# Batched row gather on one core: direct indices, six gather buffers, repeated rows left out and expanded on TensorE

## The chip, the core and the metric

The kernel runs on one core of one Trainium2 chip. A core has five engines with their own instruction queues: PE (TensorE, matrix multiplication), DVE (VectorE), ACT (ScalarE), POOL (GpSimd) and SP (SyncE), and 16 DMA engines that move data between HBM and the on-chip memory SBUF. SP, ACT and POOL can start DMA transfers; a gather by a list of row numbers is started by POOL. Matrix products land in PSUM, from which DVE and ACT copy them to SBUF. The metric is the time of one launch in microseconds (us) on the device; lower is better.

## The reference: what is computed

```python
def setup_inputs():
    batch, seq, dim = 32, 512, 1024
    return {
        "x": np.random.randn(batch, seq, dim).astype(np.float32),
        "indices": np.random.randint(0, seq, (batch, 128)).astype(np.int32),
    }

def reference(x, indices):
    for b in range(batch):
        result[b] = x[b, indices[b]]
```

For each of 32 batches, 128 rows of 1024 float32 values (4 KB each) are picked out of the batch's 512 rows and written in order. Indices are drawn with repetition, so a batch usually names some rows more than once. The launch hands the indices over as 64-bit integers. Nothing is calculated: 16.8 MB are read and 16.8 MB are written.

## The kernel before

One SBUF pool, `tp`, gives every tile name four buffers. The start: SP loads all indices transposed (L15), so that partition n holds the n-th index of every batch; these are 4096 separate elements of 8 bytes. DVE takes the low 32 bits (L17). POOL writes the row offsets 0, 512, 1024, ... with an iota (L20), and DVE adds them (L21), so that `idx2` holds row numbers in the flattened input of 32 x 512 rows.

Then a loop over the batches (L25). For each, POOL issues an indirect DMA (L27) that fetches 128 rows, one to a partition, into `buf` (128 x 1024 float32, 512 KB), and a plain DMA (L31) writes `buf` to the output. The writes alternate between SP's queue (even batches) and ACT's queue (odd batches). In the profile the gathers are queue q0, SP's DMAs q1, ACT's q10.

The tile framework derives the waits. A write waits for its gather to land. A gather waits until the write that last read its buffer, four batches earlier, has landed. Every engine goes through its queue in order, so on POOL the gather of batch 4 waits for the write of batch 0, and all later gathers stand behind it. No engine computes in the loop.

Of the kernel before, what the change touches and what calls it, by code (L numbers as in the profile page):

```python
# [5 lines left out]


@with_exitstack
def kernel(ctx, tc, x, indices, out):
    nc = tc.nc  # L10
    B, S, D = x.shape
    N = indices.shape[1]
    tp = ctx.enter_context(tc.tile_pool(name="sbuf", bufs=4))
    idx = tp.tile([128, B], dtype=indices.dtype)
    nc.sync.dma_start(out=idx[:], in_=indices[:, :].rearrange("b n -> n b"))  # L15
    idx32 = tp.tile([128, B], dtype=mybir.dt.int32)
    nc.vector.tensor_copy(out=idx32[:], in_=idx[:].bitcast(mybir.dt.int32)[:, ::2])  # L17
    idx2 = tp.tile([128, B], dtype=mybir.dt.int32)
    iota = tp.tile([128, B], dtype=mybir.dt.int32)
    nc.gpsimd.iota(iota[:], pattern=[[S, B]], base=0, channel_multiplier=0)  # L20
    nc.vector.tensor_tensor(out=idx2[:], in0=idx32[:], in1=iota[:], op=mybir.AluOpType.add)  # L21
    xf = x.flatten_outer_dims()
    of = out.flatten_outer_dims()
    engs = [nc.gpsimd, nc.sync, nc.scalar]
    for b in range(B):  # L25
        buf = tp.tile([N, D], dtype=x.dtype)
        nc.gpsimd.indirect_dma_start(  # L27
            out=buf[:], out_offset=None,
            in_=xf[:], in_offset=bass.IndirectOffsetOnAxis(ap=idx2[:, b:b+1], axis=0),
        )  # L30
        engs[1 + b % 2].dma_start(out=of[b*N:(b+1)*N], in_=buf[:])  # L31


# [1 line left out]
_INS = ['x', 'indices']  # L35
_OUTS = [((32, 128, 1024), 'float32')]


def kernel(**inputs):
    import numpy as _np  # L40
    import concourse.bacc as _bacc
    import concourse.tile as _tile
    from concourse import mybir as _mybir
    from concourse.bass_utils import run_bass_kernel_spmd as _run

    nc = _bacc.Bacc("TRN2", target_bir_lowering=False, num_devices=1)  # L46
    arrays, args = {}, []
    for name in _INS:
        a = _np.ascontiguousarray(inputs[name])
        if a.dtype.kind in "iu":  # L50
            a = a.astype(_np.int64)
        arrays[f"in_{name}_dram"] = a
        args.append(nc.dram_tensor(f"in_{name}_dram", a.shape, _mybir.dt.from_np(a.dtype), kind="ExternalInput").ap())
    for i, (shape, dtype) in enumerate(_OUTS):
        dt = _mybir.dt.from_np(_np.dtype(dtype))
        args.append(nc.dram_tensor(f"out_{i}_dram", shape, dt, kind="ExternalOutput").ap())
    with _tile.TileContext(nc) as tc:  # L57
        kernel(tc, *args)
    r = _run(nc, [arrays], core_ids=[0])
    got = tuple(r.results[0][f"out_{i}_dram"] for i in range(len(_OUTS)))  # L60
    return got[0]
```

## Time and profile before

| what | value |
|---|---|
| median of 4 runs | 112.43 us (109.51 to 113.75) |
| the profiled execution's own time | 111.54 us |
| its span, first to last instruction | 109.8 us |
| POOL busy | 30.5 us, of which 32 gathers at 943 ns |
| DVE busy | 0.4 us |
| moved by DMA | 33.60 MB, 306 GB/s over the span |
| gather, from issue to landing (median) | 6.0 us |
| write, from issue to landing (median) | 5.7 us (SP), 5.1 us (ACT) |
| index load, from issue to landing | 4.0 us |

How to read the lines that follow: "busy" counts an engine's own work, without the issuing of DMAs and without waits. In the row of DMA digits the span is cut into 40 slices, and each digit is the mean busy share of the 16 DMA engines in tenths. A DMA queue's line gives packets, megabytes, and the time its packets took as a share of 16 engines over the span; a gathered or written row of 4 KB is one packet, and each transfer ends with one small packet per DMA engine, 16 in all. A wait is named by who waited, for whom, and then total, times and longest. All of it comes from one profiled execution.

### The profile page before, as it was taken

What the parts mean: (1) busy time and instruction counts of PE and PEld (TensorE: products, weight loads), DVE (VectorE), ACT (ScalarE), POOL (GpSimd) and SP (SyncE); (2) the same over time, 40 slices, a digit from 0 to 9 for tenths busy, and PEclk for the clock granted to TensorE, in tenths of its full rate; (3) what the DMA queues carried; (4) which work ended last, traced back from release to release, by engine and by line L of the source; (5) the groups of instructions that cost most, each with busy time, mean ns of one, the idle gap of its engine ahead of it and who ended that gap; (6) DMA issues with size and microseconds to landing.
All of it is one profiled execution on the core that took longest, in us unless ns stands there. A gap on an engine that the chain in (4) does not pass through costs nothing.

```text
span 109.8 us, 173 instructions
## 1 busy us (share of the span) xinstructions
DVE 0.4 (0%) x2; POOL 30.5 (28%) x37
## 2 busy tenths in 40 slices
DVE  0100000000000000000000000000000000000000
POOL 1076003730075003720066001740037200660000
DMA  2529999899989899899989899788998999989991
GB/s 4 8 31 318 275 412 388 263 370 397 419 257 349 227 394 402 248 303 381 421 290 352 246 372 405 212 334 230 403 405 242 267 342 418 361 258 370 419 397 54
DMA packets 13329, 33.60 MB, mean 306 GB/s; under 512 B 5136, under 2 KB 5136, under 8 KB 13328
## 3 DMA queue, kind: packets, MB, share of 16 engines
q0 software_dynamic: 4608, 16.78, 48.0%
q1 hardware_dynamic: 6416, 8.42, 20.7%
q10 hardware_dynamic: 2304, 8.39, 18.7%
q14 instruction: 1, 0.01, 0.0%
HBM read 16.81 MB, written 16.78 MB: 306 GB/s over the span
## 4 chain that ended last, share of the span: by engine, by line
DMA 79%; issue 7%; POOLq 2%; POOL 1%; DVE 0%; DVEq 0%
DMA out_dram<-buf 42%; DMA buf<-in_x_dram,idx 33%; DMA idx<-in_indices_dram 4%; POOLq L57 1%; POOL buf L27 1%; DVE idx L21 0%; DVE idx L17 0%; POOLq L27 0%; DVEq L21 0%
## 5 line engine op out<-in xcount | busy, mean ns | idle before, releaser
L27 POOL DMA_INDIRECT buf<-in_x_dram,idx x32 | 30.2, 943 | 67.2 <-DMA out_dram<-buf 54.7
L20 POOL IOTA iota<- 128x32 int32 x1 | 0.1, 145 | 0.4 <-PEq L57 0.4
L17 DVE COPY idx<-idx 128x32 int32<-128x32 int32 x1 | 0.2, 181 | 4.8 <-DMA idx<-in_indices_dram 4.8
L21 DVE CUSTOM_DVE_ANT_0 idx<-idx,iota 128x64 uint16<-128x64 uint16 x1 | 0.2, 194 | 0.1
L46 POOL MEMSET const-float32-0.0<- 128x1 f32 x1 | 0.1, 100 | 0.2 <-issue 0.2
L46 POOL MEMSET const-uint8-127<- 128x1 uint8 x1 | 0.1, 120 | 0.0
L46 POOL MEMSET const-bfloat16-1.0<- 128x1 bf16 x1 | 0.1, 114 | 0.0
L46 POOL MEMSET const-float32-1.0<- 128x1 f32 x1 | 0.1, 106 | 0.0
## 6 DMA issues: line engine op xcount, KB each, us to landing
out_dram<-buf SPq DMA_DIRECT2D x16, 512.0 KB, 5.7
out_dram<-buf ACTq DMA_DIRECT2D x16, 512.0 KB, 5.1
buf<-in_x_dram,idx POOLq DMA_INDIRECT x32, 6.0
idx<-in_indices_dram SPq DMA_DIRECT2D x1, 32.0 KB, 4.0
```

Source lines behind the costliest of these rows:

```text
L17: nc.vector.tensor_copy(out=idx32[:], in_=idx[:].bitcast(mybir.dt.int32)[:, ::2])
L20: nc.gpsimd.iota(iota[:], pattern=[[S, B]], base=0, channel_multiplier=0)
L21: nc.vector.tensor_tensor(out=idx2[:], in0=idx32[:], in1=iota[:], op=mybir.AluOpType.add)
L27: nc.gpsimd.indirect_dma_start(out=buf[:], out_offset=None, in_=xf[:], in_offset=bass.IndirectOffsetOnAxis(ap=idx2[:, b:b+1], axis=0),)
L46: nc = _bacc.Bacc("TRN2", target_bir_lowering=False, num_devices=1)
L57: with _tile.TileContext(nc) as tc:
```

## The change

The changed kernel moves the same rows in another way.

- The indices are loaded in three forms. `idx0` is the first batch's list alone (128 elements). `v4` is the whole table in four quarters of 32 batches x 32 positions, two on SP's queue and two on ACT's; DVE takes the low halves (`low`) and transposes each 32 x 32 block, which gives `idxT` with a batch per column. `v` is the table with a batch per partition.
- A gather takes its row numbers straight from these; the batch's place in the input is a constant `element_offset`, so no iota of offsets is added.
- Six gather buffers `U` are used in turn. Batches 0 to 5 (`HEAD`) are gathered whole and written from `U`, alternating between SP and ACT.
- From batch 6 on, `prep` handles four batches at a time. TensorE broadcasts a batch's index list to all partitions (`bc`). DVE compares it with each partition's own index and counts equal entries at lower positions (even batches) or higher positions (odd batches) in `cnt`; `lead` marks positions whose count is zero. Other positions get 65536 added to their row number (`at`), which is out of bounds, and the gather is told to leave such rows out. `s` is a 128 x 128 matrix of zeros and ones that maps each kept row to every position that names it.
- Two matmuls of 512 columns multiply the gathered rows by `s` into PSUM (`ps`, three buffers), DVE copies the first half and ACT the second into `block`, and SP writes the block. Each of the 26 blocks has its own place in SBUF. A buffer of `U` comes free when its matmuls have read it.

The instruction order of the built program has the broadcasts of batches 6 to 25 ahead of the first expansion on PE, those of 26 to 29 after block 17 and those of 30 and 31 after block 21. ACT's copy of a block waits for DVE's. All writes from batch 6 on are in SP's queue.

```diff
--- before.py
+++ after.py
@@ -4,31 +4,125 @@
 from concourse import mybir
 from concourse._compat import with_exitstack
 
+F32 = mybir.dt.float32
+I32 = mybir.dt.int32
+ALU = mybir.AluOpType
 
 @with_exitstack
 def tile_coalesced_load_kernel(ctx, tc, x, indices, out):
     nc = tc.nc
     B, S, D = x.shape
     N = indices.shape[1]
-    tp = ctx.enter_context(tc.tile_pool(name="sbuf", bufs=4))
-    idx = tp.tile([128, B], dtype=indices.dtype)
-    nc.sync.dma_start(out=idx[:], in_=indices[:, :].rearrange("b n -> n b"))
-    idx32 = tp.tile([128, B], dtype=mybir.dt.int32)
-    nc.vector.tensor_copy(out=idx32[:], in_=idx[:].bitcast(mybir.dt.int32)[:, ::2])
-    idx2 = tp.tile([128, B], dtype=mybir.dt.int32)
-    iota = tp.tile([128, B], dtype=mybir.dt.int32)
-    nc.gpsimd.iota(iota[:], pattern=[[S, B]], base=0, channel_multiplier=0)
-    nc.vector.tensor_tensor(out=idx2[:], in0=idx32[:], in1=iota[:], op=mybir.AluOpType.add)
+    HEAD, GRP, FAR = 6, 4, 65536
+    const = ctx.enter_context(tc.tile_pool(name="const", bufs=1))
+    ring = ctx.enter_context(tc.tile_pool(name="ring", bufs=1))
+    rows = ctx.enter_context(tc.tile_pool(name="rows", bufs=1))
+    pick = ctx.enter_context(tc.tile_pool(name="pick", bufs=1))
+    junkp = ctx.enter_context(tc.tile_pool(name="junk", bufs=2))
+    pbc = ctx.enter_context(tc.tile_pool(name="pbc", bufs=2, space=bass.MemoryType.PSUM))
+    pout = ctx.enter_context(tc.tile_pool(name="pout", bufs=3, space=bass.MemoryType.PSUM))
+    idx0 = const.tile([N, 1], indices.dtype, name="idx0")
+    nc.sync.dma_start(out=idx0[:], in_=indices.rearrange("b n -> n b")[:, 0:1])
+    v4 = const.tile([N, 32], indices.dtype, name="v4")
+    for q in range(4):
+        (nc.scalar if q % 2 else nc.sync).dma_start(
+            out=v4[32 * q:32 * q + 32, :], in_=indices[:, 32 * q:32 * q + 32])
+    v = const.tile([B, N], indices.dtype, name="v")
+    nc.scalar.dma_start(out=v[:], in_=indices)
+    diff = const.tile([N, N], I32, name="diff")
+    nc.gpsimd.iota(diff[:], pattern=[[1, N]], base=0, channel_multiplier=-1)
+    idxT = const.tile([N, B], I32, name="idxT")
+    lo = v4[:].bitcast(I32).rearrange("p (n two) -> p n two", two=2)[:, :, 0]
+    low = const.tile([N, B], I32, name="low")
+    nc.vector.tensor_copy(out=low[:], in_=lo)
+    nc.vector.transpose(out=idxT[:], in_=low[:])
+    idxF = const.tile([N, B], F32, name="idxF")
+    nc.vector.tensor_copy(out=idxF[:], in_=idxT[:])
+    vf = const.tile([B, N], F32, name="vf")
+    nc.vector.tensor_copy(
+        out=vf[:], in_=v[:].bitcast(I32).rearrange("p (n two) -> p n two", two=2)[:, :, 0])
+    ident = const.tile([N, B], F32, name="ident")
+    nc.vector.tensor_scalar(out=ident[:], in0=diff[:, :B], scalar1=0, scalar2=None, op0=ALU.is_equal)
+    other = []
+    for k, op in enumerate((ALU.is_lt, ALU.is_gt)):
+        m = const.tile([N, N], F32, name=f"other{k}")
+        nc.vector.tensor_scalar(out=m[:], in0=diff[:], scalar1=0, scalar2=None, op0=op)
+        other.append(m)
     xf = x.flatten_outer_dims()
     of = out.flatten_outer_dims()
-    engs = [nc.gpsimd, nc.sync, nc.scalar]
-    for b in range(B):
-        buf = tp.tile([N, D], dtype=x.dtype)
+    def gather(dst, at, b, **kw):
         nc.gpsimd.indirect_dma_start(
-            out=buf[:], out_offset=None,
-            in_=xf[:], in_offset=bass.IndirectOffsetOnAxis(ap=idx2[:, b:b+1], axis=0),
-        )
-        engs[1 + b % 2].dma_start(out=of[b*N:(b+1)*N], in_=buf[:])
+            out=dst[:], out_offset=None,
+            in_=xf[:], in_offset=bass.IndirectOffsetOnAxis(ap=at, axis=0),
+            element_offset=b * S * D, **kw)
+    U = [ring.tile([N, D], F32, name=f"u{k}") for k in range(HEAD)]
+    for b in range(HEAD):
+        gather(U[b], idx0[:].bitcast(I32)[:, 0:1] if b == 0 else idxT[:, b:b + 1], b)
+        (nc.sync if b % 2 == 0 else nc.scalar).dma_start(out=of[b * N:(b + 1) * N], in_=U[b][:])
+    cnt = const.tile([N, B], F32, name="cnt")
+    lead = const.tile([N, B], F32, name="lead")
+    far = const.tile([N, B], F32, name="far")
+    at = const.tile([N, B], I32, name="at")
+    spread = {}
+    def prep(g0):
+        g1 = min(g0 + GRP, B)
+        bc = pbc.tile([N, GRP * N], F32, name="bc")
+        for b in range(g0, g1):
+            nc.tensor.matmul(bc[:, (b - g0) * N:(b - g0 + 1) * N],
+                             lhsT=ident[:B, b:b + 1].to_broadcast([B, N]), rhs=vf[:],
+                             start=True, stop=True)
+        for b in range(g0, g1):
+            junk = junkp.tile([N, N], F32, name="junk")
+            nc.vector.scalar_tensor_tensor(
+                out=junk[:], in0=bc[:, (b - g0) * N:(b - g0 + 1) * N], scalar=idxF[:, b:b + 1],
+                in1=other[b % 2][:], op0=ALU.is_equal, op1=ALU.mult, accum_out=cnt[:, b:b + 1])
+        w = slice(g0, g1)
+        nc.vector.tensor_scalar(out=lead[:, w], in0=cnt[:, w], scalar1=0.0, scalar2=None, op0=ALU.is_equal)
+        nc.vector.tensor_scalar(out=far[:, w], in0=cnt[:, w], scalar1=0.0, scalar2=float(FAR),
+                                op0=ALU.is_gt, op1=ALU.mult)
+        nc.vector.tensor_tensor(out=at[:, w], in0=far[:, w], in1=idxF[:, w], op=ALU.add)
+        for b in range(g0, g1):
+            s = pick.tile([N, N], F32, name=f"s{b}")
+            nc.vector.tensor_scalar(
+                out=s[:], in0=bc[:, (b - g0) * N:(b - g0 + 1) * N], scalar1=idxF[:, b:b + 1],
+                scalar2=lead[:, b:b + 1], op0=ALU.is_equal, op1=ALU.mult)
+            spread[b] = s
+    starts = list(range(HEAD, B, GRP))
+    done = 0
+    for b in range(HEAD, B):
+        while done < len(starts) and starts[done] <= b + 2 * GRP:
+            prep(starts[done])
+            done += 1
+        u = U[b % HEAD]
+        gather(u, at[:, b:b + 1], b, bounds_check=S - 1, oob_is_err=False)
+        ps = pout.tile([N, D], F32, name="ps")
+        for h in range(2):
+            nc.tensor.matmul(ps[:, h * 512:(h + 1) * 512], lhsT=spread[b][:],
+                             rhs=u[:, h * 512:(h + 1) * 512], start=True, stop=True)
+        block = rows.tile([N, D], F32, name=f"block{b}")
+        nc.vector.tensor_copy(out=block[:, :512], in_=ps[:, :512])
+        nc.scalar.copy(out=block[:, 512:], in_=ps[:, 512:])
+        nc.sync.dma_start(out=of[b * N:(b + 1) * N], in_=block[:])
 
 
 # ---- launch: one core; inputs and outputs as the reference has them ----
```

## Prediction

> **What bounds the kernel now.** I read the head of the page and its engine shares first, then the queues, the waits, and two-microsecond windows of the DMA traffic.
>
> ```profile
> span 109.8 us, 173 instructions
> ...
> DVE 0.4 (0%) x2; POOL 30.5 (28%) x37
> ...
> DMA  2529999899989899899989899788998999989991
> ...
> q0 software_dynamic: 4608, 16.78, 48.0%
> q1 hardware_dynamic: 6416, 8.42, 20.7%
> q10 hardware_dynamic: 2304, 8.39, 18.7%
> ...
> HBM read 16.81 MB, written 16.78 MB: 306 GB/s over the span
> ```
>
> No engine computes: POOL is 28% busy, and the row of DMA digits is near 9 from the fourth slice on. The DMA engines are the resource. q0 is the gathers, q1 SP's writes (and the index load), q10 ACT's writes. The same 16.78 MB cost 48.0% of the span as gathers, 52.7 us, and twice q10's 18.7%, 41.0 us, as writes. A gathered row of 4 KB took 0.480 x 109.8 x 16 / 4096 = 206 ns of a DMA engine, a written row 160 ns. Why: in the packet records of the trace both have a median of 159 ns, but 345 of the 4096 gather packets took over 300 ns; what they took above 159 ns is 174.6 us on 16 engines, 10.9 us of the span.
>
> ```profile
> POOL buf L27 <- DMA out_dram<-buf: 54.7, 9, 8.5
> POOL buf L27 <- issue: 7.9, 22, 0.6
> DVE idx L17 <- DMA idx<-in_indices_dram: 4.8, 1, 4.8
> ```
>
> These are waits: total, times, longest. POOL stands 54.7 us until a write has landed and frees one of four buffers, so four gathers go out together, then four writes. The windows (length, DVE, POOL, clock, DMA share, GB/s) show what that does:
>
> ```profile
> 10.00:12.00 2.00, 0.00 (x0) 0.45 (x1) 1.00 0.94 291
> 14.00:16.00 2.00, 0.00 (x0) 0.00 (x0) 1.00 1.02 418
> 20.00:22.00 2.00, 0.00 (x0) 1.38 (x3) 1.00 0.81 246
> 28.00:30.00 2.00, 0.00 (x0) 0.00 (x0) 1.00 1.03 420
> ```
>
> 10 to 12 is gathers alone, 291 GB/s at a share of 0.94. At 20 to 22 a new set of gathers starts: 246. 28 to 30 is writes alone, 420. The decisive one is 14 to 16; its queues:
>
> ```profile
> q0 software_dynamic: 112, 0.42, 51.4%
> q1 hardware_dynamic: 80, 0.29, 35.5%
> q10 hardware_dynamic: 30, 0.12, 14.9%
> ```
>
> Half of its bytes are gathers, the total is 418, and a gather packet took 0.514 x 2000 x 16 / 112 = 147 ns. Beside writes, gathers move at the writes' pace; alone they don't.
>
> The span: the first gather packet starts at 7.4 us, the last write packet ends 1.7 us before the end, gathers and writes take 93.7 us, so 109.8 - 7.4 - 1.7 - 93.7 = 7.0 us are holes.
>
> [...]
>
> **The change, part by part.**
>
> *Index load.* Now: issue at 0.74, 4096 packets of 8 bytes, landing at 4.79, two DVE steps, gather 0 at 5.62. After: 128 packets on SP first. The old packets started at 1.83, ran to 4.23 and landed 0.56 later; with a 32nd of the packets landing is at about 1.83 + 0.08 + 0.56 = 2.5, and gather 0 issues at 2.6, with no DVE step. Its first packet follows 1.8 us later as now (5.62 to 7.42): 4.4 instead of 7.4, minus 3.0 us. Gathers 1 to 5 need the transposed indices. The four quarter loads stand second and third on SP's queue and first and second on ACT's (0.43 us an issue), land by about 3.5, and then low, vf and transpose take three DVE steps of about 0.2 us; vf stands ahead of the transpose and waits for ACT's third load. About 4.3, against a POOL free at 2.6 + 1.39 = 4.0: cost 0 to 0.5 us, hidden by gather 0's 0.5 MB in flight.
>
> *Overlap.* Six buffers, and after the head a buffer comes free when its matmuls have read it, not when a write has landed. POOL's back-to-back pace is 1.24 us a gather (7.01 to 8.26), a block needs at least 2.5 us of DMA, so gathers run ahead and both kinds of packets are queued throughout. Gather packets then cost between 160 ns (writes' pace) and 206 ns (their present mean). I take about 178, a third of the way up, since the mixed window gave 147 but its gathers had been issued long before. Holes: bounds 0.5 and 7.0; I take 3.0, because while the first six buffers wait for their writes (gather 6 waits for write 0) there is a second short spell of gathers alone.
>
> *Skipped rows.* Counted in the input, batches 6 to 31 repeat 364 rows of 3328, so 3732 gather packets stay: 3732 x 160 / 16 = 37.3 us at least, 52.7 x 3732 / 4096 = 48.0 at most; at 178 ns 41.5. Writes stay at 41.0. [...] The bounds check on POOL is in no row: from nothing to a doubling of the 0.94 us; 2.2 us a gather still fits in a block's 2.5.
>
> *Expansion.* [...] All of this is hidden while gathers lead by six buffers and three PSUM tiles; [...] it shows once, behind the last gather, where queued writes still fill the DMA engines. New waits: PE waits for a gather with later matmuls and the last groups' broadcasts behind it; DVE's copy waits for PE with later groups' masks behind it; SP waits for ACT's copy with all later writes behind it. None is due within a block's time, as the broadcasts of batches 6 to 25 stand ahead of the first expansion.
>
> Sum: 4.4 + 41.5 + 41.0 + 3.0 + 1.2 + 1.7 = 92.8 us of span. The profiled execution took 111.54 for 109.8, 1.7 around the span: **94.5 us**. The median of the runs, 112.43, is 0.9 above the profiled one, within their spread of 4.2, so I add nothing.
>
> **Rivals.**
> *Gathers keep their own pace*, 206 ns and all holes: 4.4 + 48.0 + 41.0 + 7.0 + 1.2 + 1.7 = 103.3, 105.0 us. For it: the slow packets come with new gathers, also at 20 to 22. Against: the mixed window.
> *The skip saves nothing*, the packets being moved all the same, or POOL paying for the check: 364 packets x 178 / 16 = 4.0 more, 98.5 us. Nothing in the profile speaks on it.
> *TensorE sets the pace, cold.* Gather 0 lands at 2.6 + 4.4 = 7.0, write 0 5.7 later, gather 6 issues at 13.4 and lands at 19.4 (6.0). [...]
>
> **Chances.** 0.62 the forecast, 0.17 own pace, 0.09 no saving, 0.09 cold TensorE, 0.03 in between. Two per cent is about what a measurement of this kernel can tell from no change. Faster 0.87, same 0.04, slower 0.09. Low end: 4.4 + 37.3 + 41.0 + 0.5 + 1.2 + 1.7 = 86.1, 87.8 with the surround. High end: own pace and a little, 106; [...].
>
> **What would show it.** Right: the first gather packet near 4.4 us, GB/s digits near 400 without the swing, q0 at about 3732 plus 512 packets, POOL waiting for PE or for nothing after the head. Wrong: [...] q0's share above 46 us; q0 still at 4608 packets; POOL's gathers above 2.2 us.

## The result and the profile after

The changed kernel takes 91.9 us (median, 90.12 to 93.1) against 111.81 us for the kernel before; the ratio is 0.823, with a 95% interval of 0.812 to 0.834. The forecast was 94.5 us, with a range of 87.5 to 106.0. Medians take in a kernel's slow executions and ratios do not (the fast ones of the changed kernel took 90.1 to 91.4 us), so differences are given both ways below, a hundredth of the ratio being 1.1 us. The profiled execution took 92.8 us for a span of 90.9 us.

The page of the changed kernel: span, the rows of DMA share and of GB/s in 40 slices, and the queues.

```profile
span 90.9 us, 704 instructions
...
DMA  0189999999998998999999999999999999999760
GB/s 5 24 240 247 297 396 387 414 418 405 411 395 227 353 232 321 416 420 416 420 418 420 414 418 420 422 416 416 422 413 418 418 420 418 418 418 398 321 277 18
...
q0 software_dynamic: 4608, 15.29, 45.9%
q1 hardware_dynamic: 4416, 15.22, 41.1%
q10 hardware_dynamic: 576, 1.62, 4.5%
```

From the seventeenth slice on, the swing between 250 and 420 GB/s of the kernel before is gone: the row stands at 413 to 422 for some 45 us. Two weak places are left, the start up to 297, and a spell with 227, 353, 232 and 321 between 27 and 36 us.

In the queues, q0 carries 15.29 MB instead of 16.78. The difference, 1.49 MB, is 364 rows of 4 KB, so the skipped rows are really not moved. But q0 still has 4608 packets. In the packet records 3732 of them have 4 KB, and 876 have 4 bytes and take 9 ns: the 512 that end the transfers, as before, which leaves just one for each of the 364 skipped rows. A skipped row leaves a tiny packet in its place.

The waits of the changed kernel (who waited for whom: total, times, longest):

```profile
POOL u L70 <- PE ps L120: 24.1, 19, 2.0
...
PE ps L120 <- DMA u<-in_x_dram,at: 12.3, 15, 5.2
...
POOL u L70 <- DMA out_dram<-u: 6.2, 4, 2.9
POOL u L70 <- DVE at L102: 5.0, 1, 5.0
```

POOL's 54.7 us behind writes have become 6.2. It now waits 24.1 us for TensorE, never over 2.0 at a time: the ring of six is full, and POOL takes the next buffer as soon as matmuls have read it. Most of that costs nothing, because the DMA engines have work: 418 GB/s from 36 us on. The last line is one to distrust. It belongs to gather 6, issued at 15.27 us, and DVE had finished `at` for it at 8.44; what came last was the landing of write 0, which held the same buffer.

The windows (length, PE, weight loads, DVE, ACT, POOL, clock, DMA share, GB/s) say where the span goes:

```profile
4.00:10.00 6.00, 4.32 (x18) 4.03 (x19) 4.04 (x25) 0.00 (x0) 4.43 (x5) 1.00 0.83 225
10.00:26.00 16.00, 8.42 (x28) 5.99 (x27) 7.71 (x44) 1.28 (x1) 5.26 (x6) 1.00 1.01 397
26.00:36.00 10.00, 10.00 (x21) 4.35 (x20) 5.77 (x17) 2.43 (x5) 5.53 (x6) 1.00 0.90 291
36.00:80.00 44.00, 37.14 (x87) 13.70 (x85) 16.76 (x42) 11.02 (x19) 15.23 (x16) 1.00 1.03 418
```

At 26 to 36 us the DMA engines move 291 GB/s instead of 418. That is (418 - 291) x 10 / 418 = 3.0 us lost, while TensorE works for 10.00 of 10 us. The worst two microseconds of the spell, as a window and as its queues:

```profile
28.00:30.00 2.00, 2.00 (x4) 0.73 (x4) 0.60 (x5) 0.37 (x1) 0.99 (x1) 1.00 0.68 154
```

```profile
q0 software_dynamic: 100, 0.31, 67.9%
```

No write packet moves there, and the gather packets that do belong to gathers issued at 24.31 and 26.99 us.

### The profile page after: what moved, and what is told of

The parts are those of the page before. It is cut to its first block, busy times and chain, and to the rows that moved or that the text cites. A ratio compares the mean times of both kernels' runs of the same rounds, so it can differ in the third digit from the quotient of the medians.

```text
span 90.9 us, 704 instructions
## 1 busy us (share of the span) xinstructions
PE 64.3 (71%) x156; PEld 29.4 (32%) x156; DVE 36.9 (41%) x132; ACT 16.5 (18%) x27; POOL 32.0 (35%) x37
## 3 DMA queue, kind: packets, MB, share of 16 engines
q0 software_dynamic: 4608, 15.29, 45.9%
HBM read 16.84 MB, written 16.78 MB: 370 GB/s over the span
## 4 chain that ended last, share of the span: by engine, by line
issue 39%; DMA 34%; POOL 15%; PE 2%; DVE 2%; POOLq 1%; SPq 1%; ACT 1%; DVEq 0%
POOL u L70 15%; DMA u<-in_x_dram,at 13%; DMA u<-in_x_dram,idxT 12%; DMA out_dram<-u 7%; PE ps L120 2%; DMA v<-in_indices_dram 2%; POOLq L70 1%; DVE block L123 1%; ACT block L124 1%; SPq L39 0%; SPq L36 0%; DVE low L51 0%; POOLq L151 0%; DVE idxT L52 0%; DVE idxF L54 0%
## 5 line engine op out<-in xcount | busy, mean ns | idle before, releaser
L120 PE MATMUL ps<-u,s 128*128 128x512 f32 x104 | 52.7, 640 | 12.9 <-DMA u<-in_x_dram,at 12.3
L70 POOL DMA_INDIRECT u<-in_x_dram,at x26 | 25.7, 989 | 36.1 <-PE ps L120 24.1
L123 DVE COPY block<-ps 128x512 f32<-128x512 f32 x26 | 18.0, 691 | 41.1 <-PE ps L120 41.1
L120 PEld LDWEIGHTS ps<-u,s 128*128 128x128 f32 x104 | 19.1, 200 | 44.6 <-issue 37.1
L124 ACT COPY block<-ps 128x512 f32<-128x512 f32 x26 | 15.2, 585 | 49.4 <-DVE block L123 45.7
L90 PE MATMUL bc<-vf,ident 32*128 32x128 f32 x52 | 11.8, 398 | 8.0 <-DVE ident L59 4.4
L90 PEld LDWEIGHTS bc<-vf,ident 32*128 32x128 f32 x52 | 10.3, 291 | 10.4 <-DVE ident L59 4.4
L95 DVE SCALAR_TENSOR_TENSOR junk<-bc,idxF,other 128x128 f32<-128x128 f32 x26 | 7.9, 347 | 4.4 <-PE bc L90 4.0
L105 DVE TENSOR_SCALAR s<-bc,idxF,lead 128x128 f32<-128x128 f32 x26 | 9.5, 405 | 0.0
L70 POOL DMA_INDIRECT u<-in_x_dram,idxT x5 | 4.7, 947 | 1.7 <-issue 1.2
```

Of the source, the lines that this page charges most:

```text
L70: nc.gpsimd.indirect_dma_start(out=dst[:], out_offset=None, in_=xf[:], in_offset=bass.IndirectOffsetOnAxis(ap=at, axis=0), element_offset= ...
L90: nc.tensor.matmul(bc[:, (b - g0) * N:(b - g0 + 1) * N], lhsT=ident[:B, b:b + 1].to_broadcast([B, N]), rhs=vf[:], start=True, stop=True)
L95: nc.vector.scalar_tensor_tensor(out=junk[:], in0=bc[:, (b - g0) * N:(b - g0 + 1) * N], scalar=idxF[:, b:b + 1], in1=other[b % 2][:], op0= ...
L105: nc.vector.tensor_scalar(out=s[:], in0=bc[:, (b - g0) * N:(b - g0 + 1) * N], scalar1=idxF[:, b:b + 1], scalar2=lead[:, b:b + 1], op0=ALU. ...
L120: nc.tensor.matmul(ps[:, h * 512:(h + 1) * 512], lhsT=spread[b][:], rhs=u[:, h * 512:(h + 1) * 512], start=True, stop=True)
L123: nc.vector.tensor_copy(out=block[:, :512], in_=ps[:, :512])
```

## The experiments

My theory was the forecast's: gathers and writes queued side by side make most of the gain, the index path gives 3 us, the skipped rows give 4 us, and the expansion is hidden. The rivals: the skipped rows and the start make the gain; or gathers keep their own pace, whatever runs beside them.

**A buffer for every batch, nothing else.**

```diff
+    bp = ctx.enter_context(tc.tile_pool(name="blocks", bufs=B))
-        buf = tp.tile([N, D], dtype=x.dtype)
+        buf = bp.tile([N, D], dtype=x.dtype)
```

> The kernel before with one change: every batch has a buffer of its own, so that no gather waits for a write. If the gain is made by gathers and writes being queued side by side, gather packets fall from 205 ns to about 177 and the holes go: 7.4 + 4096 x 177 / 16000 + 40.8 + 2.4 + 1.7 = 97.6 us of span, some 99 us, ratio 0.88. If gathers keep their own pace whatever runs beside them, only the holes go: 7.4 + 52.4 + 40.8 + 2.4 + 1.7 = 104.7, some 106 us, ratio 0.95. If the gain is made by the skipped rows and the index path, no change.

Measured: 94.34 us, ratio 0.861 (0.849 to 0.874). Most of the whole gain comes from a buffer count. A gather packet takes 167 ns on average instead of 205 (packet records), less than the 177 I expected, and packets over 300 ns are down from 345 to 62. POOL no longer waits for writes; it waits 30.2 us, in 20 waits, for earlier gathers to land, with about six in flight.

**Eight buffers instead of four, nothing else.** The same edit with `bufs=8`.

> The kernel before with one change: eight gather buffers instead of four. If lead is what counts and eight suffice (a gather took 6.0 us and a write 5.7 in the kernel before, together 4.7 blocks of 2.5 us): close to the kernel with a buffer for every batch, which took 94.3 us, say 96 us, ratio 0.88. If gathers and writes still go out in turn, now eight by eight: the holes are halved and the gather packets stay slow, 105 us, ratio 0.95.

Measured: 94.33 us, ratio 0.857 (0.846 to 0.868), as fast as with a buffer for every batch. Its page and its longest wait:

```profile
span 92.3 us, 169 instructions
...
GB/s 2 13 0 206 281 261 400 398 423 419 423 419 417 417 424 424 414 423 417 423 421 417 421 421 423 419 417 417 424 421 417 421 419 423 419 419 417 423 382 21
```

```profile
POOL buf L28 <- DMA out_dram<-buf: 37.6, 23, 3.4
```

POOL still waits 37.6 us for writes, but in 23 waits of at most 3.4 us, where four buffers gave 9 waits of up to 8.5. Eight buffers let POOL issue most gathers long before their rows move: 12.4 us from issue to landing by the median, where four gave 6.0. Neither a resident output nor a skipped row is needed for this part.

Is it the writes beside them that make the gathers quick, as the forecast had it, or the time since they were issued? The packet records tell. With the packets taken in order, 144 to a gather, all 345 slow packets (over 300 ns) of the kernel before moved within 6 us of their gather's issue, and of the 83 that moved within 3 us of it beside at least two write packets in motion 67 were slow. With eight buffers, 282 gather packets moved 8 us or more after the issue with no write, or one write packet, in motion: 159 ns on average, none slow. So a gather issued long before needs no writes beside it, and a quite fresh one is slow in spite of them; what writes add for packets between 3 and 6 us is not clear from these records. Why a fresh gather has slow packets no run here shows.

**The index path alone**, with four buffers.

```diff
-    nc.sync.dma_start(out=idx[:], in_=indices[:, :].rearrange("b n -> n b"))
...
+    nc.sync.dma_start(out=idx0[:], in_=indices.rearrange("b n -> n b")[:, 0:1])
...
+    nc.vector.transpose(out=idxT[:], in_=low[:])
...
+                ap=idx0[:].bitcast(I32)[:, 0:1] if b == 0 else idxT[:, b:b + 1], axis=0),
+            element_offset=b * S * D,
```

> The kernel before with the new index path alone (first batch's list first, the others transposed on DVE, constant element offset), four buffers as before. If the start counts one to one: 3.0 us less, some 109 us, ratio 0.973. If the start is hidden or given back by the order of four gathers and four writes: no change, ratio 1.00.

Measured: 109.21 us, ratio 0.970 (0.961 to 0.979), 2.6 us less by the medians and 3.3 by the ratios. The start counts about one to one.

**Both together**, no skipping and no expansion.

> Both of the two before together: a buffer for every batch and the new index path, no row left out and nothing expanded. If the two add up: some 96 us, ratio 0.86; the skipping and expanding of the changed kernel is then worth some 4 us net. Rival: the expansion costs as much as the skipped rows save, and this kernel is as fast as the changed one, 92 us, ratio 0.82.

Measured: 91.46 us, ratio 0.833 (0.819 to 0.846). The two parts about add up, and here my theory took its first blow: this kernel, which has neither masks nor matmuls, can't be told from the changed one (0.823, 0.812 to 0.834). The difference of a hundredth lies inside the intervals. Either the skip saves nothing, or the expansion costs what it saves.

**The changed kernel without the skip.**

```diff
-    HEAD, GRP, FAR = 6, 4, 65536
+    HEAD, GRP, FAR = 6, 4, 0
```

> The changed kernel with FAR = 0: repeated rows are gathered all the same, everything else is kept, the masks, the matmuls and the copies too. If a skipped row saves its packet: 364 packets x 177 / 16000 = 4.0 us more than the changed kernel, 95.9 us. If the DMA engines are not the bound there, or a skipped row costs as much as a fetched one: no change, 91.9 us.

Measured: 94.79 us, ratio 0.859 (0.831 to 0.888): 2.9 us more than the changed kernel by the medians, 4.0 by the ratios (0.036 x 111.8). The skip does save its packets.

**The skip without the expansion.**

```diff
-        (nc.sync if b % 2 == 0 else nc.scalar).dma_start(out=of[b * N:(b + 1) * N], in_=U[b][:])
+        nc.sync.dma_start(out=of[b * N:(b + 1) * N], in_=U[b][:])
...
-        u = U[b % HEAD]
+        u = rows.tile([N, D], F32, name=f"block{b}")
+        nc.scalar.copy(out=u[:], in_=zero[:].to_broadcast([N, D]))
...
-        ps = pout.tile([N, D], F32, name="ps")
...
-        nc.sync.dma_start(out=of[b * N:(b + 1) * N], in_=block[:])
+        nc.sync.dma_start(out=of[b * N:(b + 1) * N], in_=u[:])
```

> Index lists, masks and skipped rows of the changed kernel, but every batch gathered into a buffer of its own and written from there by SP; the matmuls, the copies out of PSUM and the ring are gone. Left out: repeated rows stay zero (ScalarE puts the zeros there). If the skipped rows are worth their packets wherever the DMA engines are the bound: the kernel without skips and with a buffer for every batch, 91.5, minus 364 x 160 / 16000 = 3.6, so 87.8 us; what the changed kernel takes above it is the price of expanding, 4 us. If the skip itself costs what it saves: 91.5 us.

Measured: 88.83 us, ratio 0.801 (0.791 to 0.812). It leaves out what fills the repeated rows. The skip is worth 2.6 us by the medians against the kernel with both parts and no skip, 3.5 by the ratios, and the expansion costs 3.1 us by the medians, 2.4 by the ratios. The forecast had called it hidden. The next runs ask where it shows.

**Own buffers for the six unexpanded batches.**

```diff
...
+    for u in U:
+        nc.scalar.copy(out=u[:], in_=zero[:].to_broadcast([N, D]))
     for b in range(HEAD):
-        gather(U[b], idx0[:].bitcast(I32)[:, 0:1] if b == 0 else idxT[:, b:b + 1], b)
+        h = rows.tile([N, D], F32, name=f"block{b}")
+        gather(h, idx0[:].bitcast(I32)[:, 0:1] if b == 0 else idxT[:, b:b + 1], b)
...
```

> The changed kernel with buffers of their own for the six unexpanded batches, so that the ring of six is free when batch 6 is gathered (ScalarE fills the ring with zeros at the start, since a row left out would otherwise leave it undefined). If the slow spell at 26 to 36 us comes from gathers 6 to 11 waiting for writes 0 to 5, it goes: 3 us less, 88.8 us, ratio 0.80. If it comes from TensorE's slow first blocks, the ring fills up all the same and the spell moves earlier: no change, 91.9 us.

Measured: 90.77 us, ratio 0.819 (0.809 to 0.828). Gathers 6 to 11 now go out from 10.6 to 17.1 us without a pause, so the wait for writes is gone, and yet the time moves little, 1.1 us by the medians and 0.5 by the ratios. POOL's wait and the window:

```profile
POOL u L70 <- PE ps L125: 30.7, 18, 9.4
```

```profile
26.00:36.00 10.00, 10.00 (x23) 4.45 (x22) 5.91 (x18) 2.93 (x5) 4.94 (x5) 1.00 0.98 349
```

Most of the stall has moved, not gone: with all six ring buffers given out by 17 us, POOL stands 9.4 us until the first block has been expanded. The window is better, 349 GB/s for 291, so it loses 1.7 us instead of 3.0. The wait for writes, which the forecast had named as the cause of a second spell, was therefore at most a part of it.

**Broadcasts repeated five and ten times**, to have TensorE at work when the first gather to expand lands.

```diff
-        for b in range(g0, g1):
+        for b in [*range(g0, g1)] * (5 if g0 == HEAD + 4 * GRP else 1):
```

> The changed kernel, with the broadcasts of batches 22 to 25 done five times over, so that TensorE is kept at work from 16 us until the first expansion. If the spell comes from the cold TensorE (3.4 us for each of the first two blocks against 1.7 later): two blocks at 1.7 us less, 2 to 3 us of the span, 89.5 us. If it comes from gathers waiting for writes: no change beyond 1 us, 91 to 92 us.

> As the kernel with the repeated broadcasts, ten times instead of five, so that TensorE's work reaches to the arrival of the first gather to expand, about 23 us (with five it ended at 18.9 and TensorE was cold again). If the cold start of TensorE is what starves the spell: the first two blocks take 1.7 instead of 3.4 us, the spell is 2 to 3 us shorter, 89.5 us. If not: within 1 us of the changed kernel.

Measured: 92.43 us, ratio 0.834 (0.819 to 0.849), with five; 99.76 us, ratio 0.883 (0.874 to 0.891), with ten (10 in place of 5 in the diff). Neither answers the question. In both the instruction order left only six of the repeated broadcasts ahead of the first expansion and put the rest behind block 13. With five, TensorE stood for 4.2 us before the first expansion at 23.06, and was cold: its weight loads of 24.07 and 24.93 are 0.86 us apart, those from 28.40 on 0.43. What the run with ten shows is something else; its windows, with the clock in the third column from the right:

```profile
44.00:48.00 4.00, 4.00 (x28) 4.00 (x27) 0.00 (x0) 0.00 (x0) 0.00 (x0) 0.71 1.01 410
48.00:52.00 4.00, 4.00 (x21) 4.00 (x20) 0.00 (x0) 0.00 (x0) 0.00 (x0) 0.50 0.78 319
52.00:56.00 4.00, 4.00 (x11) 2.23 (x10) 2.59 (x15) 0.00 (x0) 0.00 (x0) 0.50 0.03 12
```

When expansion stops for 11.4 us, from 41.87 to 53.26, the DMA engines go on for some 9 us on what is queued and then stand still. And the clock falls to 0.50 while TensorE is busy without a pause: with these broadcasts, 32 rows by 128 columns with weight loads all along (4.00 of 4.00 us), it did not stay up. Behind them the weight loads of the expansion are 0.85 us apart from 54.28 to 58.55. More of these broadcasts would hardly have made the first blocks quicker.

**A ring of twelve instead of six.**

```diff
-    HEAD, GRP, FAR = 6, 4, 65536
+    HEAD, GRP, FAR, RING = 6, 4, 65536, 12
...
-    U = [ring.tile([N, D], F32, name=f"u{k}") for k in range(HEAD)]
+    U = [ring.tile([N, D], F32, name=f"u{k}") for k in range(RING)]
...
+    for u in U[HEAD:]:
+        nc.scalar.copy(out=u[:], in_=zero[:].to_broadcast([N, D]))
...
-        u = U[b % HEAD]
+        u = U[b % RING]
```

> The changed kernel with a ring of twelve gather buffers instead of six (the six that start unused are filled with zeros by ScalarE). If the slow spell at 26 to 36 us is a lack of lead, six gathers being used up before the first expanded block frees one: the spell goes, 291 to over 400 GB/s, 3 us less, 88.5 us. If it is TensorE's pace in its first blocks that holds the writes back, gathers alone fill the spell but writes are missing at the end: within 1 us of the kernel with own buffers for the unexpanded batches, 90.8 us.

Measured: 88.84 us, ratio 0.791 (0.784 to 0.797), faster than the changed kernel by 3.1 us in the medians and 3.6 by the ratios, the intervals apart. Its page, a wait and the window of the spell:

```profile
span 86.9 us, 710 instructions
...
GB/s 4 27 234 270 238 407 417 415 421 421 419 415 419 419 417 417 422 421 417 417 417 421 419 415 419 424 405 422 417 421 417 415 421 421 421 419 422 419 228 15
```

```profile
POOL u L70 <- PE ps L124: 4.0, 3, 1.5
```

```profile
26.00:36.00 10.00, 10.00 (x24) 4.31 (x23) 6.58 (x18) 2.93 (x5) 5.94 (x6) 1.00 1.03 418
```

The spell is gone, 418 GB/s, and this kernel is as fast as the one that leaves the expansion out (88.83). TensorE is as slow in its first blocks as before: its weight loads follow each other by 0.85 us from 23.27 to 26.68 us, and by 0.43 from 27.41 on. The cold start therefore does not cause the loss by itself; with lead enough it is covered.

Lead is what differs from the kernel with own buffers for the first six, which has as many buffers for gathers. There, as in the changed kernel, twelve gathers can be issued before one has to wait for an expanded block; here it is eighteen, since the buffers of the first six serve again as soon as they are written. And the spell shows once more that gathers need no writes beside them. From 27 to 30 us none move, and gathers alone, issued between 15.6 and 18.2 us, run at 419 GB/s, where the changed kernel's fresh ones ran at 154:

```profile
27.00:30.00 3.00, 3.00 (x8) 1.17 (x8) 2.12 (x11) 0.97 (x2) 2.04 (x3) 1.00 1.03 419
```

```profile
q0 software_dynamic: 384, 1.26, 103.2%
```

**Direct writing of the last two batches**, once with own buffers, written by ACT and SP, and once with the ring of twelve, written by POOL. The end of the second:

```diff
...
+    for b in range(B - TAIL, B):
+        u = U[b % RING]
+        gather(u, idxT[:, b:b + 1], b)
+    for b in range(B - TAIL, B):
+        nc.gpsimd.dma_start(out=of[b * N:(b + 1) * N], in_=U[b % RING][:])
```

> The kernel with own buffers for the six unexpanded batches, and the last two batches also gathered whole and written directly, by ACT and SP, instead of being expanded. Costs 29 more rows, 0.3 us; saves the last block's matmuls and copies (3.4 us from landing to the write's issue, 83.3 to 86.7), of which about 1.5 us at the end are not covered by other writes. Expected 1 us below the kernel with own buffers, 87.8 us; if the end is bound by the write queue: the same as that kernel.

> The kernel with the ring of twelve, and the last two batches gathered whole and written straight from the ring by POOL instead of being expanded. If the last block's matmuls and copies (3.4 us from landing to the write's issue) stand uncovered at the end: 1 to 2 us below the kernel with the ring of twelve, 87.3 us. If the queued writes cover them: the same, or 0.3 us more for the 29 rows fetched again.

Measured: 91.09 us, ratio 0.823 (0.810 to 0.835), and 89.23 us, ratio 0.792 (0.786 to 0.798). Neither gains. In the first, the direct write on ACT came ahead of the last copies in ACT's queue and held them up:

```profile
ACT block L129 <- DMA block<-in_x_dram,idxT: 9.1, 1, 9.1
```

In the second there was nothing to gain. With the ring of twelve the last 4 KB gather packet ends at 76.0 us and the last block's copy at 80.0, but queued writes keep the DMA engines busy to 85.5.

## Why the prediction was right, and where it was not

The sum for the span, term by term (packet records and timeline of the profiled execution):

| term | forecast, us | measured, us |
|---|---|---|
| first gather packet | 4.4 | 4.55 |
| gather packets | 41.5 | 41.2 |
| write packets | 41.0 | 40.8 |
| holes and uneven skips | 3.0 + 1.2 | 2.9 |
| after the last write packet | 1.7 | 1.5 |
| span | 92.8 | 90.9 |

The largest miss is in holes and uneven skips, 1.3 us; the measured 2.9 is the rest, 90.9 less the other terms, and how it divides between the two was not measured. The 1.2 us for skips that fall unevenly on the DMA engines was the author's estimate: no record here shows which engine moved which row. The profiled execution itself lies 0.9 us above the median of 91.9, and that is the other part of the 2.6 us between forecast and measurement.

*Index load.* Right: gather 0 issued at 2.75 us, 2.6 forecast, and alone the part brought 3.0%. The second gather waited 0.5 us for the transposed indices, the upper end of the bound.

*Overlap.* Right that more gathers in flight are the main part: eight buffers alone give a ratio of 0.857, 16 of the 20 us gained. The reason given for it was not right. "Beside writes, gathers move at the writes' pace; alone they don't" fits the windows of the kernel before, where gathers alone were always fresh ones. With lead they run alone at 419 GB/s, as the ring of twelve shows, and fresh ones are slow with writes beside them too. The forecast came close when it noted that the gathers of its mixed window "had been issued long before". It also misread that window: the 112 packets of q0 hold small ones as well, and the 4 KB packets took 159 ns, not 147. Nor is 178 a third of the way from 160 to 206, which is 175. In the kernels that issue gathers far ahead, the packets take 165 to 168. That the changed kernel has 176.8 is luck: its slow packets, 148 over 300 ns, fall almost all in the start and in the spell, as the records show, which the forecast had not set apart. The rival that gathers keep their own pace is refuted by the two kernels that change buffers alone.

*Skipped rows.* Right in kind: the mask saves 1.49 MB, 2.6 to 4.0 us by the two comparisons (the skip without the expansion, the changed kernel without the skip), 4.0 forecast. The rival that the skip saves nothing is out. My sign for it was wrong, though: I had written that 4608 packets in q0 would speak against the skip, and there are 4608. The bytes are what to look at. POOL's gather went from 0.94 to 0.99 us with the bounds check, next to nothing in a range up to a doubling.

*Expansion.* This step failed. Once under way, the work on a block is short enough: DVE's copy took 691 ns, ACT's 585, and four weight loads 0.43 us apart make 1.7 us of matmuls, with 2.3 us to a block (19 copies of ACT in the 44 us from 36 on). But "All of this is hidden while gathers lead by six buffers" is not what happened. Six buffers are no lead at the moment it is needed. Gathers 6 to 11 use up the ring before a block has been expanded: the first landing is followed by matmuls from 23.24 us on, at the cold pace of 0.85 us a weight load, and the first block's copies end at 28.36, so no write from a block can start before. By then the six direct writes have been made, gather 11 has been issued only at 26.99, when write 5 had freed its buffer, and gather 12 at 28.29 behind it. No write is queued, and the gathers are fresh and slow. The cost is 3.1 us by the medians and 3.6 by the ratios (the changed kernel less the one with a ring of twelve), and it takes back about what the skip saves. The forecast's holes had about this size, 3.0 us, but its reason, gather 6 waiting for write 0, was at most a part: with that wait removed the spell stayed, weaker. The kernel without the skip and the one with five times the broadcasts have the spell too, down to 267 and 271 GB/s in a slice.

*TensorE sets the pace, cold.* Outright it does not: POOL's longest wait for PE is 2.0 us, and the DMA engines are full from 36 us on. Yet the first blocks are slow. The weight loads of the changed kernel, in order of time:

```profile
27.67 0.34 PEld L120 LDWEIGHTS ps<-u,s 128*128 128x128 f32 x1 [0.52 <-issue]
28.52 0.34 PEld L120 LDWEIGHTS ps<-u,s 128*128 128x128 f32 x1 [0.52 <-issue]
29.38 0.22 PEld L120 LDWEIGHTS ps<-u,s 128*128 128x128 f32 x1 [0.52 <-issue]
29.83 0.19 PEld L120 LDWEIGHTS ps<-u,s 128*128 128x128 f32 x1 [0.24 <-issue]
30.26 0.19 PEld L120 LDWEIGHTS ps<-u,s 128*128 128x128 f32 x1 [0.24 <-issue]
```

Steps of 0.85 us, then 0.43: with four to a block (104 weight loads for 26 blocks), 3.4 us a block at first, cold as the word is meant here, and 1.7 us later, warm. What a TensorE that stays cold would cost was the author's estimate, and why it starts at half its later pace was not shown. How much of the spell of the changed kernel belongs to the cold start and how much to the ring stays open, since in the runs meant to separate them the first weight loads are about 0.85 us apart as well; the ring of twelve shows only that lead covers both.

## What to carry to other kernels

When reads and writes share the DMA engines, look at the GB/s row for a swing, and see how long before its data moves each gather was issued, before anything else is changed: here a 4 turned into an 8 is worth four fifths of a rewrite of a hundred lines. A saving in bytes on a full resource can be lost to the work added for it, if that work has no lead from its first item on: here the skip saved 3.5 us by the ratios, and the expansion took back 2.4 with a ring of six, and nothing with twelve (88.84 us, against 88.83 without the expansion). So size a ring for the first item, here 5.1 us from its first matmul to the end of its copies, and not for the steady pace, here 2.3 us a block. And a wait that is removed without gain may have moved, as POOL's did from the writes to the first expanded block, 9.4 us: look for the new longest wait on the same engine before blaming another.

## What the runs showed of the hardware that was not expected

- Gather packets were slow when they moved soon after their gather's issue, not because gathers stood alone: 205 ns on average with four buffers, 165 with eight, both with a median of 159. The difference is in packets of over 300 ns, 345 against 56, and 8 us or more after the issue those of eight buffers take 159 ns, with and without writes in motion. The cause is open.
- With a buffer for every batch, POOL stood 30.2 us waiting for its own gathers to land, with about six in flight.
- A row that the bounds check leaves out of a gather is no missing packet but one of 4 bytes that takes 9 ns. The page's figure for HBM reads did not fall with the skip (16.84 MB against 16.81 before), while q0's bytes did; why is open.
- TensorE can be busy all the time and still be slow: with the broadcasts repeated ten times its clock was 0.50 in a window of 4.00 us in which it worked for 4.00, on matmuls of 32 rows by 128 columns.
- The clock column can mislead in the other direction: it reads 1.00 at 26 to 28 us of the changed kernel, where the weight loads are 0.85 us apart, half the later pace of 0.43. The spacing is what to trust.
